# Layer 0 of a two-layer decoder trunk: plain block products on unnormalised inputs in its first two column groups, squares taken by rows, and four operand pairs of the output projection taken ahead

## The chip, the core and the metric

The kernel runs on one core of a Trainium2 chip. A core has five engines with a queue each: TensorE (PE in the profile, its weight loads PEld), VectorE (DVE), ScalarE (ACT), GpSimd (POOL) and SyncE (SP, which here only issues DMAs). Each works through its queue in order and waits on semaphores. The metric is the device time of one execution, in microseconds (us).

## The reference, cut to what matters

The input x has 1024 tokens of 1024 channels, in float32. Layer 0 normalises every token, projects to 4096 columns (2048 for pooling, 2048 for a gate), pools and mixes in four groups, gates, and projects back. Layer 1 is an attention layer that the change doesn't touch.

```python
def rms_norm(x, g):
    inv = lax.rsqrt(jnp.mean(x * x, axis=-1, keepdims=True) + RMS_EPS)
    return x * inv * g

def pooling_mixer(u, w_in, w_group, scale, w_out):
    xb, z = jnp.split(u @ w_in, 2, axis=-1)
    ...                                   # trailing means of 2, 4, 8, 16 tokens, minus self
    mixed = jnp.einsum('bsgi,gio->bsgo', pooled, w_group).reshape(B, S, D_INNER)
    return (mixed * scale * jax.nn.silu(z)) @ w_out
...
u = rms_norm(h, norm_g[0]); h = h + pooling_mixer(u, ...)
```

## The kernel before

Every float32 operand is split into a high and a low part of a faster matmul type (`split`, `u_split`): ACT copies the high part, DVE subtracts to get the low one. A 128x512 product is then three matmuls (`mm3`, lines 89 to 91): high by high, low by high, high by low.

Layer 0's input projection works on channels by tokens. The transposed x (`xt`) is cut into four blocks `B[j, l, kb]`: channel half j, token half l, and four tiles of 128 channels by 512 tokens in each. Two times 128 output columns make a `Group`; there are 16, eight for the pooled part and eight for the gate. A group is a 2 by 2 block product, done with seven block products of twelve matmuls each instead of eight, by the Strassen-Winograd scheme: the operands on the token side are `G[1]` and `G[2]` (two plain blocks of u), `G[3]` (a third) and `G[4]` to `G[7]` (sums and differences of blocks), those on the weight side are sums that POOL makes (lines 268 to 270 and 296). A sum of blocks that lie in different token halves needs u itself, with the norm factors in it.

The order at the start is therefore: `load_x(0)` loads the first token half, ACT squares each tile, TensorE adds up the squares over the channels by matmuls with a matrix of ones (line 155), POOL takes the power -1/2 (line 175), four transposes (line 178) spread the factors over the partitions, and `to_u` (line 186) multiplies. `first()` and `ahead()` then do products 1 and 2 of the four groups of the first gate and pool quarter (96 matmuls). `load_x(1)` does the second half; `u_sums` (lines 204, 205, 214, 220) makes the sums, half of them on POOL, and splits them. After that each `rest()` runs its five other products, evacuating product 1 on ACT (lines 246 and 276). Pooling (lines 314 to 323), the mixing products (`mixed`) and the stores to the DRAM tiles `yd` follow, row block by row block; the last stores go through one buffer, `old`, and POOL (lines 353 to 357).

The output projection is a 2 by 2 block product again, in a pool of tiles (`ob`) that opens when layer 0's pool closes. Its first product, `ops1`, needs `yd[1]`, complete since half of layer 0, but its loads stand behind the last stores on SP. `ops6`, the next product, needs three weight tiles per step and two sums of them on POOL (lines 452 and 453).

The Tile framework orders the instructions of each engine by a simulated timeline; the order of the code sets the priorities. PSUM has eight banks of 128x512 (`bank`).

Of the kernel before, what the change touches and what calls it, by code (L numbers as in the profile page):

```python
# [15 lines left out]
P = 128  # L16
S = 1024
# [28 lines left out]
def trunk(ctx, tc, x, xt, g, pw, pg, psc, pwo, sqk, sv, sz, swo, nf, out):  # L46
# [19 lines left out]
    ones = const.tile([P, 2], F32, name="ones")  # L66
    nc.gpsimd.memset(ones, 1.0)
# [56 lines left out]


# [6 lines left out]
    with tc.tile_pool(name="l0", bufs=2) as l0:  # L132
# [14 lines left out]
        def load_x(l, then={}):  # L147


            half = HALVES[l]  # L150
            ps = bank()

            def ssq(sq, first, last):
                for j in range(4):
                    nc.tensor.matmul(  # L155
                        ps[:, 2 * j:2 * j + 2], lhsT=sq[:, j * P:(j + 1) * P], rhs=ones,
                        start=first and j == 0, stop=last, skip_group_check=True)

            for k in range(NK):
                t = B[k // 4, l, k % 4] = pl_tile()  # L160
                nc.sync.dma_start(t, xt[k * P:(k + 1) * P, half * 512:half * 512 + 512])
                if k in then:
                    then[k]()
                sq = wide(k)[:, :512]
                act(sq, t, AF.Square)
                if l == 0:
                    ssq(sq, k == 0, k == NK - 1)
                elif k % 2:
                    nc.gpsimd.tensor_tensor(sq, sq, before, ALU.add)
                    ssq(sq, k == 1, k == NK - 1)  # L170
                before = sq
            ms = small.tile([P, 4], F32, name="ms4")
            nc.vector.tensor_scalar(ms, ps[:, 0:8:2], 1.0 / D, EPS, ALU.mult, ALU.add)
# [5 lines left out]
            rsb = l0.tile([P, 512], F32, name="w_raw", bufs=3)  # L179
            act(rsb, pt, AF.Copy)  # L180
            return rsb

        def to_u(k, l, rsb, n=None):
            j, kb = divmod(k, 4)
            t = B[j, l, kb]
            nc.vector.scalar_tensor_tensor(  # L186
                t, in0=t, scalar=g_sb[:, k:k + 1], in1=rsb, op0=ALU.mult, op1=ALU.mult)
            if n:
                u_split(n, kb, t)

        def u_split(n, kb, raw):
            hi, lo = u_tile(n, kb)
            act(hi, raw, AF.Copy)
            nc.vector.tensor_tensor(lo, raw, hi, ALU.subtract)

        def u_sums(rsb):

            t3 = []
            for kb in range(4):
                b11, b12, b22 = B[0, 0, kb], B[0, 1, kb], B[1, 1, kb]  # L200
                to_u(kb, 1, rsb)
                to_u(4 + kb, 1, rsb)
                t3.append(wide(kb)[:, :512])
                nc.vector.tensor_tensor(t3[kb], b22, b12, ALU.subtract)
                nc.gpsimd.tensor_tensor(b12, b11, b12, ALU.subtract)
                if kb:
                    t2(kb - 1, t3)
            t2(3, t3)
            for kb in range(4):
                u_split(7, kb, t3[kb])  # L210
            for kb in range(4):
                u_split(5, kb, B[0, 1, kb])
            for kb in range(4):
                nc.gpsimd.tensor_tensor(B[0, 0, kb], B[0, 0, kb], B[1, 0, kb], ALU.subtract)
                u_split(4, kb, B[0, 0, kb])
            for kb in range(4):
                u_split(3, kb, B[1, 1, kb])

        def t2(kb, t3):
            nc.vector.tensor_tensor(B[0, 0, kb], t3[kb], B[0, 0, kb], ALU.add)  # L220
            u_split(6, kb, B[0, 0, kb])
# [6 lines left out]
        def tmp():  # L228
            return l0.tile([P, 512], F32, name="avx", bufs=5)

        class Group:


            def __init__(self, c):
                self.c, self.a, self.early = c, {}, False
# [4 lines left out]
            def first(self):  # L240
                if (0, 0) not in self.a:
                    self.load(0, 0)
                self.p1 = bank()
                product(self.p1, split(self.a[0, 0]), 1)
                self.a1 = tmp()
                act(self.a1, self.p1, AF.Copy)

            def second(self):
                self.load(0, 1)
                product(self.p1, split(self.a[0, 1]), 2, True)  # L250

            def ahead(self):

                self.second()
                self.a, self.early = {}, True

            def rest(self, dst, fn):

                if self.early:
                    self.load(0, 0)  # L260
                else:
                    self.first()
# [9 lines left out]
                def out(i, l, in0, in1):  # L272
                    half = HALVES[l]
                    d = dst[i][:, half * 512:half * 512 + 512]
                    if in1 is None:
                        return act(d, in0, fn)
# [6 lines left out]
                v = self.a1  # L283
# [6 lines left out]
                if self.early:  # L290
# [607 lines left out]
```

## Time and profile before

| | us |
|---|---|
| median of 3 runs | 1623.95 (1623.34 to 1623.99) |
| the profiled execution | 1624.09 |
| its span in the trace | 1622.4 |
| PE busy | 1552.7 (96%) |
| DVE / ACT / POOL busy | 1120.4 / 674.0 / 399.6 |
| layer 0's input stage, to its last product with a token-side sum | 0 to 452 |
| output projection of layer 0 | 472 to about 640 |

PE is the busiest engine, so the time goes where PE stands idle or runs at half its clock. Views read: the share of busy time by slices, the list of what PE waited for, the timeline by engine, and tables of windows with the granted clock. A matmul's duration in the timeline overlaps its neighbours; its cost is the distance between two starts.

### The profile page before, as it was taken

To read this page: it belongs to the slowest core of one execution; us is meant where nothing else is said; L and a number is where in the kernel's file an instruction comes from. 1 tells how busy PE (TensorE), PEld (TensorE's weight loads), DVE (VectorE), ACT (ScalarE), POOL (GpSimd) and SP (SyncE) were. 2 spreads that over 40 slices of the span, in tenths; PEclk is the share of its full clock that TensorE was granted. 3 is DMA by queue.
4 is the path that set the end of the run, shared out by engine and by line. 5 is a ranking of instruction groups with operands and counts; after the bars stand their busy time and mean duration, and the time that the engine had idled before them with its cause. 6 is when DMAs were issued, how large, how long until landed. Compare 5 with 4: busy or idle time off the path is not lost.

```text
span 1622.4 us, 23428 instructions
## 1 busy us (share of the span) xinstructions
PE 1552.7 (96%) x8328; PEld 1336.8 (82%) x8328; DVE 1120.4 (69%) x1647; ACT 674.0 (42%) x1332; POOL 399.6 (25%) x826
## 2 busy tenths in 40 slices
PE   7399999999969998999999999999999999999997
PEld 7278888888857887888988988988988989989986
DVE  3597774958837687477667667657757757758678
ACT  6243332322324455355435435435335435435344
POOL 2562233254235252011102101101101102101113
PEclk9799999999979999999999999999999999999999
DMA  5113222143279742211021021021021021021012
GB/s 182 39 59 117 92 98 84 59 162 117 77 276 325 263 143 70 88 61 51 27 59 46 27 64 41 27 65 40 27 66 40 27 66 40 27 66 40 27 45 105
DMA packets 74358, 135.25 MB, mean 83 GB/s; under 512 B 8960, under 2 KB 8960, under 8 KB 74240
## 3 DMA queue, kind: packets, MB, share of 16 engines
q1 hardware_dynamic: 74096, 133.74, 25.4%
q8 instruction: 66, 1.08, 0.3%
q14 instruction: 52, 0.43, 0.1%
q10 hardware_dynamic: 144, 0.01, 0.0%
HBM read 104.35 MB, written 20.97 MB: 77 GB/s over the span
## 4 chain that ended last, share of the span: by engine, by line
PE 88%; DVE 5%; issue 2%; POOL 2%; ACT 1%; DMA 1%; SPq 0%; POOLq 0%; DVEq 0%; ACTq 0%
PE pd L89 15%; PE pd L91 14%; PE pd L90 14%; PE bk L89 10%; PE bk L90 10%; PE bk L91 10%; PE pt L727 4%; PE po L89 2%; PE po L90 2%; PE po L91 2%; PE pq L683 2%; PE pq L684 2%; PE bk L155 1%; DVE pl L186 1%; DVE w_lo L99 1%
## 5 line engine op out<-in xcount | busy, mean ns | idle before, releaser
L695 DVE TENSOR_TENSOR_SCAN om<-om 128x257 f32<-128x257 f32 (+1 forms) x192 | 187.0, 978 | 80.5 <-POOL om L692 34.6
L89 PE MATMUL pd<-slot,w_hi 128*128 128x512 f32 x512 | 202.4, 395 | 4.1 <-DVE slot L506 4.0
L90 PE MATMUL pd<-slot,w_hi 128*128 128x512 f32 x512 | 202.0, 394 | 0.0
L91 PE MATMUL pd<-slot,w_lo 128*128 128x512 f32 x512 | 200.3, 392 | 0.0
L99 DVE TENSOR_TENSOR w_lo<-w_raw,w_hi 128x512 fp32r<-128x512 f32 x196 | 141.3, 728 | 82.1 <-ACT w_hi L98 77.9
L98 ACT ACTIVATE w_hi<-w_raw 128x512 fp32r<-128x512 f32 x196 | 122.4, 629 | 135.4 <-PE pd L90 77.6
L688 ACT ACTIVATE om<-pq 128x256 f32<-128x256 f32 (+1 forms) x192 | 94.3, 491 | 169.0 <-PE pq L684 162.1
L89 PE MATMUL pd<-w_hi,slot 128*128 128x256 f32 x512 | 146.3, 286 | 0.0
L91 PE MATMUL pd<-w_hi,slot 128*128 128x256 f32 x512 | 144.6, 283 | 0.0
L90 PE MATMUL pd<-w_lo,slot 128*128 128x256 f32 x512 | 144.3, 282 | 0.0
L692 POOL TENSOR_SCALAR_AFFINE_SELECT om<-om 128x128 f32<-128x128 f32 x128 | 48.8, 384 | 374.5 <-ACT om L688 371.8
L98 ACT ACTIVATE w_hi<-a_raw 128x512 fp32r<-128x512 f32 x96 | 59.8, 629 | 150.1 <-PE bk L90 88.0
L89 PEld LDWEIGHTS pd<-slot,w_hi 128*128 128x128 f32 x512 | 96.6, 189 | 22.7 <-DVE slot L506 4.3
L731 DVE TENSOR_TENSOR at_l<-pt,at_h 128x512 fp32r<-128x512 f32 (+1 forms) x160 | 99.4, 625 | 21.1 <-ACT at_h L730 20.9
L730 ACT ACTIVATE at_h<-pt 128x512 fp32r<-128x512 f32 (+1 forms) x160 | 86.6, 552 | 63.8 <-PE pt L727 63.1
L91 PEld LDWEIGHTS pd<-slot,w_lo 128*128 128x128 f32 x512 | 96.6, 189 | 19.9 <-DVE w_lo L99 0.4
L90 PEld LDWEIGHTS pd<-slot,w_hi 128*128 128x128 f32 x512 | 96.6, 189 | 18.4
L699 DVE TENSOR_TENSOR om<-pq,om 128x256 f32<-128x256 f32 (+1 forms) x192 | 104.7, 551 | 9.0 <-DVE t L753 0.2
L89 PE MATMUL pd<-w_hi,y_h 128*128 128x512 f32 x256 | 107.0, 418 | 0.4 <-ACT y_h L756 0.4
L99 DVE TENSOR_TENSOR w_lo<-a_raw,w_hi 128x512 fp32r<-128x512 f32 x96 | 75.4, 788 | 39.1 <-ACT w_hi L98 39.1
L90 PE MATMUL pd<-w_lo,y_h 128*128 128x512 f32 x256 | 102.1, 399 | 0.0
L91 PE MATMUL pd<-w_hi,y_l 128*128 128x512 f32 x256 | 100.3, 395 | 0.0
(185 smaller groups left out, 4043.3 us busy)
## 6 DMA issues: line engine op xcount, KB each, us to landing
a_raw<-in_pw SPq DMA_DIRECT2D x72, 256.0 KB, 3.0
w_raw<-in_pwo SPq DMA_DIRECT2D x72, 256.0 KB, 4.6
y_raw<-y_dram SPq DMA_DIRECT2D x56, 256.0 KB, 4.0
y_dram<-t SPq DMA_DIRECT2D x48, 256.0 KB, 2.1
w_raw<-in_sqk SPq DMA_DIRECT2D x34, 256.0 KB, 2.8
w_raw<-in_sz SPq DMA_DIRECT2D x34, 256.0 KB, 3.2
w_raw<-in_sv SPq DMA_DIRECT2D x32, 256.0 KB, 2.7
w_raw<-in_swo SPq DMA_DIRECT2D x32, 256.0 KB, 2.6
```

The costliest lines, as they stand in the source:

```text
L89: nc.tensor.matmul(ps, lhsT=lh, rhs=rh, start=start, stop=False, skip_group_check=more)
L90: nc.tensor.matmul(ps, lhsT=lh, rhs=rl, start=False, stop=False, skip_group_check=more)
L91: nc.tensor.matmul(ps, lhsT=ll, rhs=rh, start=False, stop=stop, skip_group_check=more)
L98: act(hi, raw, AF.Copy)
L99: nc.vector.tensor_tensor(lo, raw, hi, ALU.subtract)
L688: act(om[:, 1:1 + n], pz, AF.Sigmoid, scale=-ZSCALE)
L692: nc.gpsimd.affine_select(out=om[:, 1:1 + P], in_=om[:, 1:1 + P], pattern=[[1, P]], base=0, channel_multiplier=-1, compare_op=ALU.is_gt, f ...
L695: nc.vector.tensor_tensor_scan(out=om[:, :1 + n], data0=om[:, :1 + n], data1=om[:, :1 + n], initial=1.0 if s.first else carry[r], op0=ALU. ...
L699: nc.vector.tensor_tensor(om[:, :n], pz, om[:, :n], ALU.mult)
L727: nc.tensor.transpose(tp[:, c * P:(c + 1) * P], om[:, (j - b0) * P:(j - b0 + 1) * P], ident)
L730: act(ah[:, :n], tp[:, :n], AF.Copy)
L731: nc.vector.tensor_tensor(al[:, :n], tp[:, :n], ah[:, :n], ALU.subtract)
```

## The change

- The first two groups, `Group(0)` (pool) and `Group(16)` (gate), are done as eight plain block products, four column tiles `c1` on the first token half and four (`c2`) on the second. They take `xt` times the weight `g` of each channel, without the norm factors; the factors are put on when the result leaves PSUM (`scaled`, on DVE). The weights of these groups stay split in tiles that `G[5]` and `G[7]` take over later; the second half's operands stand in `G[4]` and `G[3]` until the true ones come.
- `G[1]` and `G[2]` stay without norm factors for all groups. Product 1 is evacuated by DVE with a multiplication by the factors `rsb[0]` instead of by ACT as a copy, and so is the result of products 1 and 2.
- The sums of squares are taken from x by rows, with ACT's accumulator (`factors`), in place of 96 small matmuls with ones; the four x tiles of each half are loaded a second time for that, 512 KB each.
- The sums of `u_sums` are all made on DVE, none on POOL.
- Half of the first product of the output projection (row blocks 0 to 3, 48 matmuls) is done inside layer 0's last quarter.

```diff
+        def factors(l):
+            ssq = small.tile([P, 4], F32, name="ssq4")
+            for j in range(4):
+                t = wide(j)[:, :D]
+                nc.sync.dma_start(t, xv[4 * HALVES[l] + j])
+                act(t, t, AF.Square, accum_out=ssq[:, j:j + 1])
             rs = small.tile([P, 4], F32, name="rs4")
-            nc.gpsimd.tensor_tensor(rs, ms, mhalf.broadcast_to([P, 4]), ALU.pow)
+            nc.gpsimd.tensor_scalar(rs, ssq, 1.0 / D, EPS, ALU.mult, ALU.add)
+            nc.gpsimd.tensor_tensor(rs, rs, mhalf.broadcast_to([P, 4]), ALU.pow)
             pt = bank()
             for j in range(4):
                 nc.tensor.transpose(pt[:, j * P:(j + 1) * P], rs[:, j:j + 1].broadcast_to([P, P]), ident)
...
+        def scaled(d, ps, l, fn):
+            d = d[:, HALVES[l] * 512:HALVES[l] * 512 + 512]
+            nc.vector.tensor_tensor(d, ps, rsb[l], ALU.mult)
+            if fn != AF.Copy:
+                act(d, d, fn)
...
-                    self.first()
+                self.load(0, 0)
+                p1 = bank()
+                product(p1, split(self.a[0, 0]), 1)
+                v = tmp()
+                nc.vector.tensor_tensor(v, p1, rsb[0], ALU.mult)
...
+        c1 = {(a, i): bank() for a in range(2) for i in range(2)}
+        for j in range(2):
+            first_w(j)
+            for k in range(4 * j, 4 * j + 4):
+                for a, i in c1:
+                    first_mm(c1[a, i], a, i, k, (1, 2))
+        factors(0)
+        for k in range(NK):
+            load_xt(k, 1, (4, 3)[k // 4])
+        factors(1)
+        c2 = {}
+        for a in range(2):
+            for i in range(2):
+                ps = c2[a, i] = bank()
+                for k in range(NK):
+                    first_mm(ps, a, i, k, (4, 3))
...
+                if gi == 3 and op == 1:
+                    y1 = []
+                    for kb in range(4):
+                        t = wide(kb)
+                        raw, hi = t[:, :512], t[:, 512:S].bitcast(F32R)
+                        nc.sync.dma_start(raw, yd[1][kb])
+                        split_to((hi, raw.bitcast(F32R)), raw)
+                        y1.append((hi, raw.bitcast(F32R)))
...
+                    if gi == 3 and op + i == 2:
+                        pa = [bank() for _ in range(4)]
+                        out_product(pa, lambda kb: (
+                            split(raw_of(pwo[kb][:, :512], l0, "a_raw", bufs=6)), y1[kb]), kbs=range(4))
                     mixed(gi, 2 * op + i, pooled, dst[i])
...
-        out_product(pa, ops1)
+        out_product(pa, ops1, kbs=range(4, 8))
```

In numbers of large matmuls (128x512), layer 0's input and mixing stages had 16 x 84 + 768 = 2112 and now have 14 x 84 + 2 x 96 + 768 = 2136; the 96 with ones are gone.

**PE's queue where the factors of the second token half come in.** Before, the transposes of the second half's factors (`rs_455`) follow the 96 products of `first` and `ahead` and some of the matmuls with ones, and the next product takes the sums of u (`g_0h` is here a part of `G[6]` or `G[7]`):

```order
L90 MATMUL bk<-g_3l,w_hi 128x512
L91 MATMUL bk<-g_3h,w_lo 128x512
L155 MATMUL bk<-ones,xb 128x2 x5
L178 MATMUL bk<-ident,rs_455 128x128 x4
L89 MATMUL bk<-g_0h,w_hi 128x512 x2
L90 MATMUL bk<-g_0l,w_hi 128x512
```

Now the factors of both halves are transposed behind the 96 products of `c1`, and the next product is the first of the 96 of `c2`, on `xt` alone:

```order
L88 MATMUL bk<-g_3l,g_3h 128x512
L89 MATMUL bk<-g_3h,g_3l 128x512
L184 MATMUL bk<-ident,rs_335 128x128 x4
L184 MATMUL bk<-ident,rs_406 128x128 x4
L87 MATMUL bk<-g_0h 128x512
L88 MATMUL bk<-g_0l,g_0h 128x512
```

So 192 large matmuls stand ahead of the first one that needs u, where 96 stood; `c2` itself needs no factor but stands behind the transposes of `rs_406`.

**DVE's queue up to the first weight split of the next group.** `w_lo<-a_raw` is the low part of a weight sum that product 6 waits for; before, the sums of u alternate with their splits (L194), and half of them come from POOL:

```order
L220 TENSOR_TENSOR pl<-xb,pl 128x512
L194 TENSOR_TENSOR g_3l<-pl,g_3h 128x512
L194 TENSOR_TENSOR g_0l<-pl,g_0h 128x512
L194 TENSOR_TENSOR g_1l<-pl,g_1h 128x512
L194 TENSOR_TENSOR g_2l<-pl,g_2h 128x512
L194 TENSOR_TENSOR g_3l<-pl,g_3h 128x512
L99 TENSOR_TENSOR w_lo<-a_raw,w_hi 128x512 x2
```

Now the same queue holds the evacuations of `c1` and `c2` (L207), pooling of the first two tiles (L273 to L276) and the sums on u (L369 to L371, L387) as well:

```order
L276 SCALAR_TENSOR_TENSOR wsum<-wsum,xb 128x1024
L157 TENSOR_TENSOR g_3l<-pl,g_3h 128x512
L157 TENSOR_TENSOR g_2l<-pl,g_2h 128x512
L387 TENSOR_TENSOR pl<-pl 128x512
L157 TENSOR_TENSOR g_0l<-pl,g_0h 128x512
L157 TENSOR_TENSOR g_1l<-pl,g_1h 128x512
L275 TENSOR_TENSOR wsum<-wsum,ratio_82 128x1
L207 TENSOR_TENSOR t_570<-bk,w_raw 128x512
L157 TENSOR_TENSOR g_2l<-pl,g_2h 128x512
L387 TENSOR_TENSOR pl<-pl 128x512
L97 TENSOR_TENSOR w_lo<-a_raw,w_hi 128x512
```

That `w_lo`, the last row, now stands 58 instructions behind the first multiplication of x by the factors.

**PE's queue at the end of layer 0.** Before, the rest of the mixing products (`pl`) stands behind the last product with `G[3]`, 23 matmuls to the first one of the output projection:

```order
L90 MATMUL bk<-g_3l,w_hi 128x512
L91 MATMUL bk<-g_3h,w_lo 128x512
L91 MATMUL bk<-pl,w_lo 128x512 x2
L89 MATMUL bk<-pl,w_hi 128x512
L90 MATMUL bk<-pl,w_hi 128x512
L91 MATMUL bk<-pl,w_lo 128x512
```

Now the products taken ahead (`wsum` and `xb` hold their row blocks) follow it, 27 of the 48, and then 24 mixing products; the other 21 stand in front of it:

```order
L87 MATMUL bk<-g_3h,w_hi 128x512
L88 MATMUL bk<-g_3l,w_hi 128x512
L89 MATMUL bk<-g_3h,w_lo 128x512
L87 MATMUL bk<-w_hi,wsum 128x512
L88 MATMUL bk<-w_lo,wsum 128x512
L89 MATMUL bk<-w_hi,wsum 128x512
L87 MATMUL bk<-w_hi,xb 128x512
```

51 products in place of 23 stand between the last product with `G[3]` and the first one on loads of the output projection.

## Rows read from the trace of the kernel before

**Rows 1.** The page's busy times; what PE waited for, 0 to 560 us.
```profile
PE 1552.7 (96%) x8328; PEld 1336.8 (82%) x8328; DVE 1120.4 (69%) x1647; ACT 674.0 (42%) x1332; POOL 399.6 (25%) x826
...
PE bk L89 <- ACT g_0h L193: 27.6, 2, 25.5
```

**Rows 2.** Timeline of PE: start, duration, instruction, count, idle before.
```profile
4.89 1.84 PE L155 MATMUL bk<-ones,wsum 128*128 128x2 f32 x8 [4.89 <-ACT wsum L165]
...
33.28 0.63 PE L89 MATMUL bk<-g_1h,w_hi 128*128 128x512 f32 x1
33.70 0.63 PE L90 MATMUL bk<-g_1l,w_hi 128*128 128x512 f32 x1
...
55.44 0.65 PE L178 MATMUL bk<-ident,rs 128*128 128x128 f32 x4 [1.36 <-POOL rs L175]
81.57 1.22 PE L89 MATMUL bk<-g_0h,w_hi 128*128 128x512 f32 x2 [25.48 <-ACT g_0h L193]
...
85.58 0.40 PE L90 MATMUL bk<-g_0l,w_hi 128*128 128x512 f32 x1
```

**Rows 3.** Windows: length, busy by engine, granted clock, DMA share, GB/s.
```profile
10.00:15.00 5.00, 5.00 (x25) 5.00 (x25) 2.06 (x3) 3.48 (x6) 0.00 (x0) 1.00 1.05 395
...
55.00:60.00 5.00, 0.65 (x4) 0.41 (x4) 3.25 (x2) 0.60 (x1) 4.76 (x5) 0.83 0.00 0
60.00:65.00 5.00, 0.00 (x0) 0.00 (x0) 5.00 (x7) 3.10 (x6) 1.29 (x1) 0.50 0.01 2
```

**Rows 4.** Timeline of ACT at the start.
```profile
4.14 0.61 ACT L165 ACTIVATE wsum<-pl 128x512 f32<-128x512 f32 x1
...
15.94 0.63 ACT L165 ACTIVATE wsum<-pl 128x512 f32<-128x512 f32 x1 [2.17 <-DMA pl<-in_xt]
```

**Rows 5.** Timeline of POOL, 18 to 106 us.
```profile
18.96 1.03 POOL L175 TENSOR_TENSOR rs<-ms,mhalf 128x4 f32<-128x4 f32 x1 [0.35 <-DVE ms L173]
...
65.83 11.16 POOL L205 TENSOR_TENSOR pl<-pl 128x512 f32<-128x512 f32 x3 [4.54 <-DVE wsum L204]
```

**Rows 6.** Timeline of DVE, 18 to 125 us.
```profile
21.83 5.39 DVE L186 SCALAR_TENSOR_TENSOR pl<-pl,g_sb,w_raw 128x512 f32<-128x512 f32 x8 [2.95 <-ACT w_raw L180]
...
65.67 0.68 DVE L194 TENSOR_TENSOR g_0l<-pl,g_0h 128x512 fp32r<-128x512 f32 x1
66.28 0.68 DVE L204 TENSOR_TENSOR xb<-pl 128x512 f32<-128x512 f32 x1
...
75.80 1.75 DVE L194 TENSOR_TENSOR g_0l<-wsum,g_0h 128x512 fp32r<-128x512 f32 x1
77.47 1.75 DVE L194 TENSOR_TENSOR g_1l<-xb,g_1h 128x512 fp32r<-128x512 f32 x1
...
108.12 2.34 DVE L314 TENSOR_TENSOR wsum<-xb 128x1024 f32<-128x1024 f32 x2
...
111.17 4.59 DVE L317 SCALAR_TENSOR_TENSOR wsum<-wsum,xb 128x1024 f32<-128x1024 f32 x2
```

**Rows 7.** PE's first and last large matmul of the stretch without a wait.
```profile
122.92 0.50 PE L89 MATMUL bk<-g_0h,w_hi 128*128 128x512 f32 x1 [0.28 <-DVE avx L287]
...
452.05 0.39 PE L91 MATMUL bk<-g_3h,w_lo 128*128 128x512 f32 x1
```

**Rows 8.** Window of 40 us with the busiest DVE, columns as in rows 3.
```profile
280.00:320.00 40.00, 40.00 (x178) 33.14 (x177) 38.50 (x45) 14.53 (x26) 14.07 (x11) 1.00 0.21 66
```

**Rows 9.** Timeline, all engines, from the last product to the output projection.
```profile
466.73 0.42 SPq L104 DMA_DIRECT2D w_raw<-in_pwo  x1
...
471.96 2.07 PE L89 MATMUL bk<-w_hi,y_hi 128*128 128x512 f32 x4 [14.31 <-ACT y_hi L98]
```

**Rows 10.** The output projection's first product and `ops6`: window, POOL's sums, PE's wait.
```profile
500.00:505.00 5.00, 5.00 (x23) 3.83 (x21) 2.78 (x4) 2.05 (x4) 1.73 (x3) 1.00 1.05 388
...
518.26 1.62 POOL L453 TENSOR_TENSOR s<-s,w_raw 128x512 f32<-128x512 f32 x1
...
506.71 1.21 PE L89 MATMUL bk<-w_hi,y_hi 128*128 128x512 f32 x4 [1.67 <-ACT w_hi L98]
```

More of the change, by code (lines that the diff above doesn't have):

```diff
@@ L123, in trunk, with out_product @@
     HALVES = (1, 0)
+    def out_product(ps, operands, more=False, kbs=range(8)):
+        for kb in kbs:
+            (wh, wl), (yh, yl) = operands(kb)
+            for t in range(4):
+                ts_ = slice(t * P, (t + 1) * P)
+                mm3(ps[t], yh[:, ts_], yl[:, ts_], wh, wl, kb == 0 and not more, kb == 7, more)
     ps_ctx = ExitStack()
@@ L145, in wide, with split_to @@
             return l0.tile([P, S + 16], F32, name="xb" if i % 2 else "wsum")
[L147 to L173, printed above, removed]
+        def split_to(t, raw, scale=None):
+            hi, lo = t
+            if scale is None:
+                act(hi, raw, AF.Copy)
+                nc.vector.tensor_tensor(lo, raw, hi, ALU.subtract)
+            else:
+                act(hi, raw, AF.Copy, scale=scale)
+                nc.vector.scalar_tensor_tensor(lo, in0=raw, scalar=scale, in1=hi, op0=ALU.mult, op1=ALU.subtract)
@@ L186, in to_u @@
             nc.vector.scalar_tensor_tensor(
-                t, in0=t, scalar=g_sb[:, k:k + 1], in1=rsb, op0=ALU.mult, op1=ALU.mult)
-            if n:
-                u_split(n, kb, t)
+                t, in0=t, scalar=g_sb[:, k:k + 1], in1=rsb[l], op0=ALU.mult, op1=ALU.mult)
         def u_split(n, kb, raw):
[L192 to L221, printed above, removed]
+            split_to(u_tile(n, kb), raw)
         def product(ps, w, n, more=False):
@@ L289, in rest @@
                 out(1, 1, x_, p5)
-                if self.early:
-                    self.load(0, 1)
-                else:
-                    self.second()
-                out(0, 0, self.p1, None)
+                self.load(0, 1)
+                product(p1, split(self.a[0, 1]), 2, True)
+                scaled(dst[0], p1, 0, fn)
                 a12 = self.a[0, 1]
@@ new lines, in trunk, with first_w @@
+        fw = {}
+        def first_w(j):
+            for a, c in enumerate(first):
+                for i in range(2):
+                    raw = raw_of(pw[c + i][:, j * 512:j * 512 + 512], l0, "a_raw", bufs=6)
+                    n = (7, 5)[a]
+                    t = fw[a, i, j] = tuple(
+                        l0.tile([P, 512], F32R, name=f"g{n}_{2 * i + j}{x_}", bufs=1) for x_ in "hl")
+                    split_to(t, raw)
+                    if j == 0:
+                        load_xt(2 * a + i, 0, 1)
+                    else:
+                        load_xt(4 + 2 * a + i, 0, 2)
@@ L375, in trunk @@
+        for kb in range(4):
+            dve(B[0, 0, kb], B[0, 0, kb], B[1, 0, kb], ALU.subtract)
+            u_split(4, kb, B[0, 0, kb])
+        for kb in range(4):
+            u_split(3, kb, B[1, 1, kb])
         for gi in range(len(WINDOWS)):
             pooled = {}
-            if gi:
-                xs = [Group(gi * 4), Group(gi * 4 + 2)]
-                zs = [Group(16 + gi * 4), Group(16 + gi * 4 + 2)]
             for cp in range(2):
-                dst = [xb_tile() for _ in range(2)]
-                xs[cp].rest(dst, AF.Copy)
+                if gi + cp:
+                    dst = [xb_tile("old" if gi == 0 and i else "xb", 2 - (gi == 0 and i)) for i in range(2)]
+                    Group(gi * 4 + 2 * cp).rest(dst, AF.Copy)
+                else:
+                    dst = firsts[0]
@@ L411, in ysplit @@
             return split(raw_of(yd[n][kb], ob, "y_raw"), ob, "y")
-        def out_product(ps, operands, more=False):
-            for kb in range(8):
-                (wh, wl), (yh, yl) = operands(kb)
-                for t in range(4):
-                    ts_ = slice(t * P, (t + 1) * P)
-                    mm3(ps[t], yh[:, ts_], yl[:, ts_], wh, wl, kb == 0 and not more, kb == 7, more)
         def tmp2(name):
@@ L438, in ops1 @@
             return split(wload(0, 0, kb)), ysplit(1, kb)
-        pa = [bank() for _ in range(4)]
-        out_product(pa, ops1)
+        out_product(pa, ops1, kbs=range(4, 8))
         a1 = []
```

97 lines of the change are left out of this document (51 added, 46 removed).

## The prediction, made before the changed kernel ran

> **What bounds the kernel now.** I read the busy times first: PE is busy 96% of the span [rows 1], so the change can only win where PE stands idle, runs at half clock, or does matmuls that go away. The list of waits shows where that is: PE loses 27.6 us to the first split of u, 25.5 of it in one wait [rows 1], and 14.3 us to the first operand of the output projection [rows 9]; between 122.92 and 452.05 it has no wait worth a term. PE's timeline tells the start: sums of squares from 4.89 on, 96 large products up to about 54 (55.44 less the 1.36 of its wait), and then nothing until 81.57, while DVE and POOL make the sums of u [rows 2]. The reader should see three paces there: a large matmul every 0.43 us at the half clock (from 33.28 to 33.70) [rows 2], every 0.227 us at the full one (1450 matmuls by the order between 122.92 and 452.05, 329.13 / 1450) [rows 7], and a granted clock that falls to 0.50 soon after PE stops (0.83 in the 5 us in which it stops) and comes back about 4 us after it resumes [rows 2, 3]. DVE has two paces as well: 0.61 us from start to start alone, 1.67 us while POOL adds tiles (the three of 11.16 us and the ones behind them) [rows 5, 6].
>
> **The first products (gain).** They need a weight tile, an x tile and their splits, no factor. ACT can start at 4.14 [rows 4]; two copies of 0.63 give PE a start near 5.5. The 16 tiles have 256 KB each; before, the 17th tile of that size is there at 15.94 [rows 4], so the last lands near 15, and ACT (0.63 a copy) and DVE (0.61) keep up. PE is the slower: about 12 products at half clock (5 us), then 84 x 0.227 = 19.1. I put the end of `c1` at 30.
>
> **The wait for the factors (loss).** `c2` stands behind the transposes of both factors. The x tiles by rows are the last of 40 times 256 KB: 17 by 15.9, the other 23 at 395 GB/s [rows 3], 0.66 each, so about 31. ACT, in order, waits with three of the four squares behind the copy of the first factors, which waits for transposes behind `c1`. So from 30: transposes 0.65 [rows 2], copy 0.6, three squares, POOL's power 1.03 [rows 5] and a small multiplication, transposes 0.65. A 128x1024 square with the accumulator isn't shown; between the 0.63 of a 128x512 one [rows 4] and twice that plus a read of the accumulator lies 0.6 to 1.45; I take 1.3, since the time of such copies goes with their columns, so 3.9 (1.9 to 4.4). With handoffs 7.3: `c2` starts at 37.3, at half clock, as after the stop at 54. 96 x 0.227 = 21.8 and about 2.2 for ten products at half clock: its end is 61.5. The ones-matmuls that go, from 4.89 on [rows 2], lay where PE had nothing else; that gain is in the start at 5.5 and isn't counted again.
>
> **DVE's queue (where the stall goes).** PE could go on at 61.5, but the weight split `w_lo` of product 6 is late. From the first multiplication by factors, at 31.3, to the weight split that the mixing of the first group needs stand 80 DVE instructions: 16 with a scalar at 0.67 (5.39 for 8), four of 1024 columns at 1.17 to 2.3 (I take 1.2, since the larger one ran beside POOL), two tiny of 0.2, and 58 at 0.60 [rows 6]: 10.7 + 4.8 + 0.4 + 34.8 = 50.7. Seven weight sums on POOL lie in that stretch; at 1.67 for the instructions that they slow, against 0.61, I add half of seven times 1.06, 3.6 (0 to 7.4). DVE is there at 85.6. PE waits for it about 5 us at product 6, runs some products at half clock again, waits 1 to 2 us more before the mixing, and has done its 282nd large product by 91. The first rival says what it is without DVE.
>
> [...]
>
> **The rest of layer 0.** By the order of before, the 255th large product starts at 122.92 and the 1705th, the last with `G[3]`, at 452.05. Now the 283rd starts at 91 and the 1749th is 1466 x 0.227 = 332.8 later: 423.8, a gain of 28.3, with the 24 added products and the 21 taken ahead paid in it. 14 groups put two evacuations each on DVE that ACT did: 28 x 0.6 = 17 us of DVE's time, hidden where DVE is idle. It is 38.5 of 40 us busy at worst [rows 8]; two groups a stretch of that length put in 2.4, so there they overflow by about 1. I take 1.5 lost (0 to 8).
>
> **The output projection.** The chain behind the last `G[3]` product doesn't change: silu, scale, POOL, store, reload through `old`, POOL, and only then SP's loads, 14.7 us after it (466.73), and PE's first product, 19.9 after it (471.96) [rows 7, 9]. 51 products, 11.6 us, fill that time in place of 23; the last mixing products are done before POOL wants them, so the chain isn't longer. After it 48 products fewer are left, 10.9 us. But that stage is fed by DMA: 388 GB/s in `ops6`, with PE waiting for its weight sums (1.67 us) [rows 10], and POOL's last sum ends at 519.9, 53.2 us after the first load. With four steps less, 8 loads of 256 KB go, 2.1 MB, 5.4 us at 388 GB/s; POOL's and PE's work comes earlier by no more than this. So 5.4 is the ceiling, not 10.9; with PE waiting more, and cooler, I take 4.5 (0 to 6).
>
> **The sum.** 28.3 - 1.5 + 4.5 = 31.3 off the profiled execution's 1624.09 gives 1592.8; the median of the runs lies 0.14 lower: **1592.6**.
>
> **Rivals.** *DVE doesn't hold PE:* the multiplications and splits keep ahead, and the 90 products behind `c2` run from 61.5 at 0.227, to 82 in place of 91: 1583.6. For it: PE's own order has 18 products between `c2` and the first need; against: 58 instructions in front of it. *DVE holds it longer:* 1.67 us for more than seven instructions and 2.3 for the wide ones, or the weight loads late behind `a_raw` tiles that hold sums of u until DVE has read them (SP waits there in order): 12 us more, 1604.6. *The output projection gains nothing*, since what it waits for is DMA and POOL: 1597.1, inside the main range. *Slower:* product 1 is evacuated by DVE in order, and PE, which adds product 2 onto the same bank, waits for it; with a wide operation in front (2.3 us) [rows 6] at each of 28 evacuations, 64 us are lost, 1656. It decides from 1.2 us per evacuation on (32.8 / 28). Against it: PE does 36 products, 8 us, between the two, and it waited for DVE nowhere in this stretch with DVE at 38.5 of 40 [rows 8]. *The change doesn't do what it says:* PE's work can't start before the factors anyway. The order speaks against it, since `c1` stands first on PE.
>
> **How the numbers follow.** Forecast, with the output projection's rival inside it: 0.66. DVE not holding: 0.12. DVE holding longer: 0.15. Slower: 0.03. No start ahead of the factors, near 1620: 0.04, half within 0.2%. The range is the forecast with the bounds of its terms: low 1592.6 - 9 (no hold by DVE) - 1.5 - 0.9 = 1581; high 1592.6 + 4 + 6.5 + 1.4 = 1604.5 with half of the longer hold inside. About 0.2% (3.2 us) is what a measurement of this kernel can tell from no change. Faster 0.95, same 0.02, slower 0.03.
>
> **What would show it right or wrong.** In the profile after: PE's first large matmul near 5.5, `c1` ended near 30, a gap of 6 to 7 us with eight transposes, `c2` from 37 to 61, a wait of some 5 us on `w_lo` near 66 to 71, no PE wait of length from 95 to 424, a gap of 8 us before the output projection, and PE waits in `ops6`. It is wrong if PE is idle beyond 95, if waits on lines 226 or 207 show up between 100 and 420, or if `ops6` ends more than 6 us earlier or later against the last `G[3]` product than I put it.

## The result, and the profile of the changed kernel

The changed kernel takes 1601.74 us (median of 4 runs, 1599.34 to 1602.63) against 1623.64 in the same rounds: a ratio of 0.9866, with an interval of 0.9848 to 0.9883. That is 21.9 us less, where 31.3 was forecast; the time lies in the upper part of the range. The profiled execution took 1599.34 us (span 1597.3), 24.75 less than the profiled execution before, and the steps are judged on that pair. It is the changed kernel's fastest execution, 2.4 us below its median, so the pair shows 2.9 us more than the medians do.

What PE waited for up to 700 us (in total, times, longest), as in [rows 1]:

```profile
PE bk L87 <- ACT y_hi L96: 14.1, 1, 14.1
PE bk L87 <- ACT w_hi L96: 10.3, 4, 4.2
PE bk L184 <- POOL rs L181: 6.3, 1, 6.3
PE bk L87 <- ACT g_0h L159: 5.4, 1, 5.4
PE bk L89 <- DVE w_lo L97: 5.4, 1, 5.4
PE pd L87 <- ACT w_hi L96: 2.3, 1, 2.3
```

The 25.5 us behind the sums of u have become three shorter waits (6.3, 5.4 and 4.2, the last one inside the second line). The first line is the gap ahead of the output projection, as long as before [rows 9]. The other three waits of the second line lie in the output projection, where one of 1.7 stood before [rows 10].

PE's timeline in the same form as [rows 2] and [rows 7]: its first large product, the last one of `c2`, the waits, the last product with `G[3]`, the output projection, the last transposes, layer 1:

```profile
5.44 0.80 PE L87 MATMUL bk<-g_0h 128*128 128x512 f32 x1 [5.44 <-ACT g_0h L159]
...
36.44 1.12 PE L184 MATMUL bk<-ident,rs 128*128 128x128 f32 x4 [6.33 <-POOL rs L181]
...
60.33 0.39 PE L89 MATMUL bk<-g_3h,g_3l 128*128 128x512 f32 x1
...
70.62 0.80 PE L89 MATMUL bk<-g_0h,w_lo 128*128 128x512 f32 x1 [5.41 <-DVE w_lo L97]
...
86.46 0.80 PE L87 MATMUL bk<-pl,w_hi 128*128 128x512 f32 x1 [4.24 <-ACT w_hi L96]
...
95.75 0.39 PE L89 MATMUL bk<-pl,w_lo 128*128 128x512 f32 x1
...
429.14 0.39 PE L89 MATMUL bk<-g_3h,w_lo 128*128 128x512 f32 x1
...
455.33 2.07 PE L87 MATMUL bk<-w_hi,y_hi 128*128 128x512 f32 x4 [14.12 <-ACT y_hi L96]
...
616.72 5.80 PE L525 MATMUL bk<-ident,s 128*128 128x128 f32 x32 [2.12 <-DVE s L521]
...
624.78 0.50 PE L87 MATMUL pd<-slot,w_hi 128*128 128x512 f32 x1 [2.26 <-ACT w_hi L96]
```

Up to 82 us this is the forecast. The wait at 86.46 is not in it. In the windows of the waits at 70.62 and 86.46 the granted clock was 0.55 and 0.50 (columns as in [rows 3]):

```profile
70.00:75.00 5.00, 4.38 (x11) 3.53 (x12) 5.00 (x9) 1.89 (x3) 0.00 (x0) 0.55 0.29 89
...
85.00:90.00 5.00, 3.54 (x8) 2.81 (x9) 4.08 (x7) 2.19 (x4) 0.23 (x1) 0.50 0.49 168
```

The last transposes and the first product of layer 1 in the kernel before:

```profile
638.10 5.80 PE L501 MATMUL bk<-ident,s 128*128 128x128 f32 x32 [2.12 <-DVE s L497]
...
647.93 0.50 PE L89 MATMUL pd<-slot,w_hi 128*128 128x512 f32 x1 [4.03 <-DVE slot L506]
```

So the gain at the last product with `G[3]` is 452.05 - 429.14 = 22.9, at the last 32 transposes 638.10 - 616.72 = 21.4, and at the first product of layer 1 647.93 - 624.78 = 23.2. From the `G[3]` product to the transposes the change *lost* 1.5 us; behind them it won 3.4, which no step spoke of.

### The profile page after: what moved, and what is told of

Same layout as the page of the kernel before. It is cut to its first block, busy times and chain, and to the rows that moved or that the text cites. A ratio compares the mean times of both kernels' runs of the same rounds, so it can differ in the third digit from the quotient of the medians.

```text
span 1597.3 us, 23281 instructions
## 1 busy us (share of the span) xinstructions
PE 1539.7 (96%) x8256; PEld 1322.8 (83%) x8256; DVE 1131.8 (71%) x1681; ACT 663.1 (42%) x1310; POOL 362.6 (23%) x807
## 3 DMA queue, kind: packets, MB, share of 16 engines
q8 instruction: 65, 1.06, 0.3%
## 4 chain that ended last, share of the span: by engine, by line
PE 67%; DMA 4%; DVE 3%; POOL 1%; ACT 1%; issue 1%; SPq 0%; POOLq 0%; DVEq 0%; ACTq 0%
PE pd L89 15%; PE pd L87 15%; PE pd L88 15%; PE pt L751 4%; PE bk L88 3%; PE bk L89 2%; PE bk L87 2%; PE po L87 2%; PE po L88 2%; PE po L89 2%; PE pq L707 2%; PE pq L708 2%; DMA w_raw<-in_pwo 1%; DVE wsum L273 1%; DMA y_raw<-y_dram 1%
## 5 line engine op out<-in xcount | busy, mean ns | idle before, releaser
L97 DVE TENSOR_TENSOR w_lo<-w_raw,w_hi 128x512 fp32r<-128x512 f32 x190 | 135.7, 722 | 77.4 <-ACT w_hi L96 72.8
L96 ACT ACTIVATE w_hi<-w_raw 128x512 fp32r<-128x512 f32 x190 | 118.6, 628 | 141.1 <-PE pd L88 74.1
L96 ACT ACTIVATE w_hi<-a_raw 128x512 fp32r<-128x512 f32 x88 | 54.6, 628 | 151.8 <-PE bk L88 90.2
L88 PEld LDWEIGHTS pd<-w_lo,slot 128*128 128x128 f32 x512 | 97.5, 190 | 0.8
```

The lines of the kernel that those rows point to most:

```text
L88: nc.tensor.matmul(ps, lhsT=lh, rhs=rl, start=False, stop=False, skip_group_check=more)
```

## The experiments

The table has the medians of the timed runs, the ratio to the kernel before, and four landmarks of the profiled execution: the 283rd large product, the last product with `G[3]`, the last block of transposes, and the first product of layer 1. Between executions of equal code the landmarks move by one to three us (the last product with `G[3]` stands at 429.14 in the changed kernel and at 427.58 in e9, which differs from it behind that place only; at 423.62 in e8 and 426.79 in e10), so late landmarks are compared by their distances. The last product with `G[3]` is not the same place everywhere: it is the 1705th large product before and in e5, with 23 more up to the output projection, the 1744th in e1, e6 and e11, with 8 more, and the 1749th in the others, with 51 more. A distance from it holds different work in each of the three.

| kernel | median us | ratio (interval) | 283rd | last `G[3]` | transposes | layer 1 |
|---|---|---|---|---|---|---|
| before | 1623.6 | | | 452.05 | 638.10 | 647.93 |
| changed | 1601.74 | 0.9866 (0.9848 to 0.9883) | 95.75 | 429.14 | 616.72 | 624.78 |
| e1 | 1605.67 | 0.9888 (0.9872 to 0.9905) | 96.85 | 429.33 | 617.67 | 631.91 |
| e2 | 1603.30 | 0.9877 (0.9863 to 0.9892) | 95.41 | 428.21 | 612.68 | 626.89 |
| e3 | 1593.93 | 0.9816 (0.9801 to 0.9830) | 91.03 | 424.33 | 609.86 | 617.92 |
| e4 | 1598.63 | 0.9847 (0.9833 to 0.9862) | 92.71 | 425.97 | 616.13 | 624.19 |
| e5 | 1621.23 | 0.9990 (0.9981 to 0.9998) | | 450.36 | 636.07 | 644.13 |
| e6 | 1600.68 | 0.9862 (0.9848 to 0.9875) | 95.51 | 427.18 | 616.12 | 624.19 |
| e7 | 1592.57 | 0.9811 (0.9798 to 0.9824) | 90.11 | 424.56 | 608.94 | 617.01 |
| e8 | 1585.84 | 0.9771 (0.9758 to 0.9784) | 89.19 | 423.62 | 602.03 | 610.11 |
| e9 | 1601.45 | 0.9866 (0.9853 to 0.9880) | 94.84 | 427.58 | 617.67 | 626.00 |
| e10 | 1587.52 | 0.9782 (0.9769 to 0.9796) | 91.59 | 426.79 | 606.55 | 614.61 |
| e11 | 1589.02 | 0.9789 (0.9776 to 0.9802) | 89.99 | 423.27 | 603.93 | 612.01 |
| e12 | 1597.99 | 0.9848 (0.9835 to 0.9862) | 94.52 | 428.28 | 613.30 | 623.14 |

### The start: what made the wait at 86.46 (e3, e4, e7, e12)

What SP's queue waited for in the changed kernel between 20 and 100 us, longest first:

```profile
SPq L102 <- DVE pl L371: 28.6, 4, 27.2
SPq L102 <- DVE t L207: 11.9, 1, 11.9
SPq L102 <- DVE w_lo L97: 11.3, 5, 5.5
```

SP stood 27.2 us before one weight load, until DVE had read the first tile of `t3` for the last time (line 371): `t3` lies in tiles of `a_raw`. Behind it SP stood another 11.9 us, before a load into the tile `w_raw` that holds the second half's factors until line 207 has read them. The loads for the next weight sums went out from 73.04 on, and POOL and ACT show what came of it:

```profile
76.21 5.68 POOL L232 TENSOR_TENSOR w_raw<-a_raw 128x512 f32<-128x512 f32 x1 [10.95 <-DMA a_raw<-in_pw]
81.97 1.59 POOL L233 TENSOR_TENSOR a_raw<-a_raw 128x512 f32<-128x512 f32 x1
...
83.57 1.66 POOL L255 TENSOR_TENSOR a_raw<-a_raw 128x512 f32<-128x512 f32 x1
```

```profile
85.26 0.63 ACT L96 ACTIVATE w_hi<-a_raw 128x512 fp32r<-128x512 f32 x1 [6.29 <-POOL a_raw L255]
85.79 1.13 ACT L96 ACTIVATE w_hi<-w_raw 128x512 fp32r<-128x512 f32 x2
```

PE wanted the second row's split, of a weight tile with no sum in it, but ACT works in order and waited 6.29 us for the sum of the first row. DVE itself was through its list at 84.1.

**e3: `t3` in other tiles.**

```diff
-            t3.append(l0.tile([P, 512], F32, name="a_raw", bufs=6))
+            t3.append(tmp())
```

> The changed kernel, with the four sums t3 in the tiles avx, so that SP can load the next groups' weights into a_raw while DVE still reads t3. If the wait of 4.2 us before the first mixing product (86.46) comes from weight loads that stand behind t3's tiles: that wait goes, with the half clock behind it, the next group's 283rd large product starts near 91 in place of 95.5, and the time is 4 to 5 us shorter. If DVE's queue alone holds PE there, PE's wait is as long as before, the 283rd large product within 1 us of 95.5, and the time the same.

The 283rd large product starts at 91.03, the forecast's 91 (94.84 to 96.85 in the changed kernel and the four with its start: e1, e2, e6, e9), and the median falls by 7.8 us, where 4 to 5 had been expected. What PE still waited for from 60 to 100 us:

```profile
PE bk L89 <- DVE w_lo L97: 1.2, 1, 1.2
PE bk L88 <- DVE g_3l L157: 0.9, 1, 0.9
PE bk L87 <- ACT w_hi L96: 0.4, 1, 0.4
```

The first theory holds. It cost something too: SP puts weight loads in front of the last x tiles, so the second transposes come at 40.42 in place of 36.44. The profiled executions differ by 7.2 us. 4.8 of them are there at the last `G[3]` product and 2.1 come between it and the transposes, where PE's waits in the output projection are 5.6 us in place of 7.2; whether the edit or the spread between executions makes these 2.1, no run shows.

**e4: the transposes of the second half's factors inside `c2`.**

```diff
...
                 ps = c2[a, i] = bank()
                 for k in range(NK):
                     first_mm(ps, a, i, k, (4, 3))
+                if a + i == 0:
+                    spread(1, rs1)
```

> The changed kernel, with the transposes of the second half's factors behind the first 24 matmuls of c2 instead of in front of all of them, so that PE has work while ACT squares and POOL takes the power. If DVE's queue sets when layer 0 gets going (the prediction's step): c2 ends 6 us earlier, near 54, PE then waits as much longer for the weight split of product 6, and the 283rd large product starts within 1 us of 95.5. If PE is what binds, it starts 6 us earlier and the time is 6 us shorter.

Neither held. `c2` ends at 52, 8.4 us earlier, and PE then waits 9.1 us in one piece in place of 5.4, for ACT's copy of a weight tile; the 283rd product comes 3.0 us earlier. ACT's queue has that copy behind one of a sum of u, which DVE had ready at 64.0, and POOL's weight sum, whose load had waited 30.4 us for the tiles of `t3`, was done at 63.4. This run can't tell DVE and the loads apart; e7 can.

**e7: e2, e3 and e4 together.** (e2 stands below.)

> The changed kernel with the edits of e2, e3 and e4 together: products taken ahead behind the last mixing, t3 in other tiles, transposes of the second half's factors inside c2. Layer 1's first product takes bank 0, freed by the third of the eight transposed tiles, as in the changed kernel. If the three gains lie in different places: e3's 7.8 us, 3 us of e4, and e2's 4 us at the transposes add up to 13 to 15 us, near 1587. If DVE's queue is what holds layer 0's start once the loads are early, e4's part goes under: PE waits again for a split behind c2, and the time is near 1590.

The second theory held, and e2's part went under too: from the 283rd product to the transposes e7 and e3 both need 518.8 us. The last matmul of `c2` starts at 59.87 where it starts at 63.98 in e3, but PE then waits 3.2 us for the split of `g_0h`, and the last `G[3]` product is at 424.56 against 424.33. ACT's copy in that split had waited for a sum on DVE (line 376). DVE is the reason, in a window of e7 (columns as in [rows 3]):

```profile
50.00:90.00 40.00, 34.92 (x136) 26.75 (x135) 40.00 (x62) 17.89 (x31) 10.74 (x6) 0.91 0.15 46
```

DVE is busy 40.00 of 40 us with 62 instructions. With the loads early, DVE's list is the bound of this stretch, as the prediction said.

**e12: as e7, with four of the sums of u on POOL, as before the change.**

```diff
-        dve(B[0, 0, kb], B[0, 0, kb], B[1, 0, kb], ALU.subtract)
+        nc.gpsimd.tensor_tensor(B[0, 0, kb], B[0, 0, kb], B[1, 0, kb], ALU.subtract)
```

> As e7, with the last four sums of u (those for G[4]) on POOL, as before the change, instead of on DVE. DVE is busy without a break from 50 to 90 us in e3 and e7. If DVE's count of instructions sets the pace: four less are 2.4 us, so the last product with G[3] comes up to 2.4 us earlier. If POOL's sums slow DVE by 1.06 us each (1.67 for 0.61, as in the kernel before): 4.2 us more than gained 2.4, so about 2 us later, and POOL's weight sums come later as well.

The last `G[3]` product comes 3.7 us later than in e7, the 283rd product at 94.52, where it starts at 89.19 to 91.59 in the four kernels with the sums on DVE (e7, e8, e10, e11). That is the second theory, with more lost than its 2 us. The same window, and DVE and POOL beside each other, in e12:

```profile
50.00:90.00 40.00, 31.76 (x122) 24.41 (x121) 40.00 (x55) 17.95 (x31) 16.10 (x9) 0.88 0.12 40
```

```profile
41.40 1.27 POOL L235 TENSOR_TENSOR w_raw<-a_raw 128x512 f32<-128x512 f32 x1
...
69.68 5.20 POOL L235 TENSOR_TENSOR w_raw<-a_raw 128x512 f32<-128x512 f32 x1 [12.60 <-DVE t L210]
74.95 2.29 POOL L236 TENSOR_TENSOR a_raw<-a_raw 128x512 f32<-128x512 f32 x1
...
77.25 5.07 POOL L392 TENSOR_TENSOR pl<-pl 128x512 f32<-128x512 f32 x3
```

```profile
76.02 0.68 DVE L229 TENSOR_TENSOR avx<-bk,rsb 128x512 f32<-128x512 f32 x1
...
77.72 1.77 DVE L157 TENSOR_TENSOR g_2l<-pl,g_2h 128x512 fp32r<-128x512 f32 x1
79.42 1.78 DVE L97 TENSOR_TENSOR w_lo<-a_raw,w_hi 128x512 fp32r<-128x512 f32 x1
```

DVE is as busy as in e7, but gets through 55 instructions in place of 62: four of them, beside POOL's sums of u, took 1.75 to 1.78 us in place of 0.68. The other way round, POOL's sum at 69.68 took 5.20 us while DVE kept its pace, 0.68 to 0.69 an instruction. The number of inputs in SBUF doesn't tell here which instruction is slowed: beside POOL's sum at 74.95 the evacuation at 76.02, which reads PSUM and one tile in SBUF, took 0.68, and a DVE instruction with two inputs in SBUF at 75.42 took 0.68 as well. What decides whether DVE or POOL is slowed was not shown. The median is 5.4 us above e7; about 2 of them are a wait at layer 1 (4.0 in place of 2.3, below).

### The end of layer 0 and the output projection (e1, e2, e6, e8 to e11)

**e1: nothing taken ahead.**

```diff
-                        pa = [bank() for _ in range(4)]
-                        out_product(pa, lambda kb: (
-                            split(raw_of(pwo[kb][:, :512], l0, "a_raw", bufs=6)), y1[kb]), kbs=range(4))
...
-        out_product(pa, ops1, kbs=range(4, 8))
+        pa = [bank() for _ in range(4)]
+        out_product(pa, ops1)
```

> The changed kernel, but all eight steps of the output projection's first product stand behind layer 0, as before; nothing is taken ahead. The prediction's step (taking ahead gains 4.5 us): the transposes behind the output projection start 4 to 5 us later than the 616.7 us of the changed kernel, and the time is about 1606. The theory from the changed kernel's trace: taking ahead lost there, since its 48 matmuls stand in front of the last mixing products and lengthen the chain from the last product with G[3] to SP's loads (21.1 us against 14.7 before). Then without it the last product with G[3] comes 21 x 0.227 = 4.8 us earlier, at 424.4, the first product of the output projection 20 to 23 us behind it, near 446, and the transposes 166 us behind that, near 612: 3 to 6 us faster than the changed kernel.

Neither theory held. The last `G[3]` product stands at 429.33 and not at 424.4: only 5 large products fewer come in front of it, not 21, since the scheduler moved mixing products there. The time, 3.9 us up, looks like the prediction's 4.5. The landmarks say otherwise: the transposes are only 1 us later, and the rest is a longer wait in front of layer 1's first product, 8.42 us in place of 2.26:

```profile
631.91 0.80 PE L87 MATMUL pd<-slot,w_hi 128*128 128x512 f32 x1 [8.42 <-DVE slot L518]
```

This product doesn't need the tile that it waits for here. By the program's allocation it takes PSUM bank 0 over from the pool that closes, and the eight last transposed tiles rotate through the banks: in e1 bank 0 is read last by the eighth of them, in the kernel before by the fifth, in the changed kernel by the third. Which one it is depends on the order in which banks were taken all through layer 0. The traces agree: the product starts at 631.91 in e1, where the eighth evacuation ends at 631.86, and at 647.93 in the kernel before, where the fifth ends at 647.87.

**e5: the kernel before, and e6: e1, each with layer 1's pools opened in another order,** so that the first product takes bank 1, which the first of the eight tiles frees.

```diff
+    ps_o = ctx.enter_context(tc.tile_pool(name="ps_o", bufs=1, space=PSUM, reuse_waits="tile"))
     ps_d = ctx.enter_context(tc.tile_pool(name="ps_d", bufs=3, space=PSUM, reuse_waits="tile"))
...
-    ps_o = ctx.enter_context(tc.tile_pool(name="ps_o", bufs=1, space=PSUM, reuse_waits="tile"))
```

> The kernel before, with one line moved: the pool of one bank (ps_o) is opened ahead of ps_d, so that layer 1's first product pd lies in bank 1 instead of bank 0. Bank 0 is read last by the fifth of the eight last transposed tiles, bank 1 by the first of them. If layer 1's first product waits for the evacuation of the bank that it takes over: its wait of 4.0 us falls to the 2.3 us that its weight split needs, as in the changed kernel, PE doesn't fall to the half clock behind it, and the time is 2 to 4 us shorter than before. If the wait is for its operands, nothing changes.

> As e1 (nothing of the output projection taken ahead), with ps_o opened ahead of ps_d: layer 1's first product then takes bank 1, which the first of the eight last transposed tiles frees, in place of bank 0, which the last of them frees. If e1's wait of 8.4 us there comes from the bank: it falls to 2.3, and the time is 6 to 7 us shorter than e1. What is left against the changed kernel is then what taking ahead is worth by itself: the transposes stood 1 us later in e1, so within 1 to 2 us of the changed kernel; by the prediction's step 4.5 us slower than it.

Layer 1's first product in e5 and in e6:

```profile
644.13 0.50 PE L89 MATMUL pd<-slot,w_hi 128*128 128x512 f32 x1 [2.26 <-ACT w_hi L98]
```

```profile
624.19 0.80 PE L87 MATMUL pd<-slot,w_hi 128*128 128x512 f32 x1 [2.27 <-ACT w_hi L96]
```

Both fall to 2.3 us. The kernel before gains 2.1 us by the median (its interval ends at 0.9998), e1 gains 5.0 (6 to 7 had been expected). So the bank theory holds, and e6, with nothing taken ahead, stands at 1600.68 against 1601.74: taking ahead is worth nothing that can be measured in this kernel. From the 283rd large product to the transposes, the same work in both, e6 needs 520.6 us and the changed kernel 521.0. The 48 products taken ahead bring the output projection's first product 6.4 us later (359.6 us behind the 283rd in place of 353.2) and shorten the way from it to the transposes by 6.1 us (161.4 in place of 167.5), not by the 10.9 us of their work.

**e2: the products taken ahead behind the last mixing products.**

```diff
                 for i in range(2):
-                    if gi == 3 and op + i == 2:
-                        pa = [bank() for _ in range(4)]
...
                     mixed(gi, 2 * op + i, pooled, dst[i])
+                if gi == 3 and op == 1:
+                    pa = [bank() for _ in range(4)]
+                    out_product(pa, lambda kb: (
```

> The changed kernel, with the 48 matmuls taken ahead placed behind the last mixing products instead of in front of them. If the order of PE's queue alone lengthened the chain: the last product with G[3] at 424.4, SP's loads 14.7 us behind it (439) in place of 450.2, the gap of PE before the output projection about 9 us in place of 14.1, and the time 8 to 11 us shorter. If the chain of stores through the one old buffer and the two t buffers sets the pace whatever PE does (four row blocks at 8 to 9 us each): loads 5 to 6 us earlier and the time about as much shorter. If the output projection is fed by DMA alone, as the prediction said, the waits in ops6 stay (7 us in the changed kernel).

The first product of the output projection comes 25.1 us behind the last `G[3]` product, where the changed kernel has 26.2 and the kernel before 19.9. So the place in PE's queue accounts for 1.1 of the 6.3 us by which the chain grew, and none of the times expected came. PE's waits in `ops6` stay, at 6.0 us, as the third theory said. The transposes are 4.0 us earlier than in the changed kernel; the wait of 8.4 us at layer 1 (bank 0 is freed by the eighth tile here as well) takes that back.

Part of the rest shows on DVE at the end of layer 0. The changed kernel first, then the kernel before:

```profile
432.82 0.69 DVE L207 TENSOR_TENSOR t<-bk,rsb 128x512 f32<-128x512 f32 x1 [6.06 <-DMA y_dram<-t]
```

```profile
452.54 0.69 DVE L277 TENSOR_TENSOR t<-bk,avx 128x512 f32<-128x512 f32 x1 [6.14 <-PE bk L91]
```

Before, the last group's evacuation waits for PE; now it waits 6.06 us for a store, since its tile `t` is one of two and the row block two places earlier isn't out. The chain through `old` (POOL, store, reload, POOL) sets the end; moving PE's last products changes it by 1.0 us (e2). From POOL's first step of the last four row blocks to the output projection it takes 34.3 us before (437.67 to 471.96), 34.9 in e1 (415.40 to 450.33), 37.4 in e2 and 38.4 in the changed kernel (416.94 to 455.33). The 2.5 to 3.5 us that taking ahead adds to e1's time lie in several small waits; a single cause wasn't found.

**e8: as e7, with the loads of x for the residual held back.**

```diff
+        if after is not None:
+            nc.vector.tensor_copy(h[t, n][:, :1], after[:, :1])
         nc.sync.dma_start(h[t, n], xv[t][:, n * 512:n * 512 + 512])
...
-            load_h(t, 0)
+            load_h(t, 0, v[0])
...
```

> As e7, with twelve loads of x for the residual (256 KB each) held back by a one-column DVE write until ops6 has ended; in the changed kernel they lie between 459 and 477 us, between the weights of ops6. If DMA feeds ops6, as the prediction said: 12 x 256 KB are 3.1 MB, 8 us at 388 GB/s; the waits in ops6 (7 us and a half clock behind them in the changed kernel) fall to under 2 us, and the time is 5 to 8 us shorter than e7. If POOL's sums or the store of the last rows bind there, it is the same within 2 us.

6.7 us faster than e7, as the first theory said. PE's waits from 440 to 560 us, in e7 and in e8:

```profile
PE bk L87 <- ACT w_hi L96: 5.0, 2, 3.3
PE bk L88 <- DVE w_lo L97: 1.3, 2, 0.6
```

```profile
PE bk L88 <- DVE w_lo L97: 1.1, 3, 0.4
PE bk L87 <- ACT w_hi L96: 1.0, 1, 1.0
```

The same window of both, e7 first (columns as in [rows 3]; the last one is what DMA moved, in GB/s):

```profile
460.00:465.00 5.00, 5.00 (x24) 4.14 (x23) 3.26 (x4) 3.84 (x7) 2.95 (x2) 1.00 1.06 388
```

```profile
460.00:465.00 5.00, 5.00 (x24) 4.14 (x23) 4.39 (x5) 3.92 (x9) 3.47 (x3) 1.00 0.76 210
```

From 460 to 480 us DMA moved 386 GB/s in e7, about as much as the 388 in [rows 10], and 295 in e8. So DMA feeds `ops6`, and 12 loads that nobody needs yet took 3.1 MB of it. Whether their bytes cost the time or their places between the weight loads in SP's queue, the run doesn't separate. At 1585.84 us e8 is the fastest kernel of the study, 15.9 us below the changed one.

**e9: ops1's loads on ACT's queue; e10: the same on e8; e11: e10 with nothing taken ahead.** (e11 has the first four steps' loads on ACT's queue.)

```diff
...
-            return split(wload(0, 0, kb)), ysplit(1, kb)
+            return split(wload(0, 0, kb, nc.scalar)), ysplit(1, kb, nc.scalar)
```

> The changed kernel with one thing moved: the eight loads of ops1 (weights and yd[1]) are issued from ACT's queue instead of SP's, where they stand behind the last stores of layer 0. yd[1] is complete since half of layer 0. If the gap of 14.1 us before the output projection comes from the order of SP's queue: ACT is free of the last evacuations at 434.8, the loads go out there instead of at 450.2, ops1 follows the last mixing product (440.8) with a gap under 3 us, and the time is 5 to 10 us shorter, the rest going into ops6, whose operands still come behind the stores. If the tiles of ob can't be had before layer 0's last tiles are free, the gap stays.

> As e8 (products behind the last mixing, t3 apart, transposes inside c2, x loads late), with ops1's eight loads on ACT's queue as in e9. If both hold: the gap of 12.9 us before the output projection shrinks below 4, ops6 starts as early as its own operands allow, near 449, and the time is 5 to 9 us shorter than e8's 1585.8, near 1579.

> As e10, but with nothing of the output projection taken ahead: all eight steps of ops1 stand behind layer 0, the first four steps' loads on ACT's queue. If taking ahead only fills a gap that the order of SP's queue makes, 96 products (21.8 us) fill the same time, and the time is within 2 us of e10. If it is worth the 4.5 us of the prediction by itself, because 16 loads less stand in the DMA-fed stage, it is 4 us or more slower than e10.

e9 keeps the gap (15.1 us) and the time, but it is no clean test of SP's order: SP now issues seven loads of x from 448.46 on, while `ops1`'s last operands are still to come. In e10 the loads of x are held back; the gap is 11.3 us where e8 has 12.9, and PE's waits in `ops6` grow from 2.1 to 5.1 us. So the order of SP's queue accounts for at most 1.6 us of the gap, which had been expected to fall below 4. The gap in e10:

```profile
450.35 2.07 PE L87 MATMUL bk<-w_hi,y_hi 128*128 128x512 f32 x4 [11.32 <-ACT y_hi L96]
```

In e9 ACT's last evacuation starts at 432.66, but its loads go out late and one by one:

```profile
440.77 0.33 ACTq L102 DMA_DIRECT2D w_raw<-in_pwo  x1
444.57 0.34 ACTq L102 DMA_DIRECT2D y_raw<-y_dram  x1
446.29 0.33 ACTq L102 DMA_DIRECT2D w_raw<-in_pwo  x1
```

The tiles of the output projection lie on tiles of layer 0 (by the allocation, `y_raw` on the `wsum` and `xb` that hold the row blocks taken ahead), which fits the second theory; which tile each load waited for wasn't settled. e10 and e11 stand 1.5 us apart, within e10's "within 2 us": a second time taking ahead is worth at most that. e10 is no faster than e8, where 5 to 9 us had been expected.

## Why the prediction was right in its sign and 9 us too low

- **First products.** Right: PE starts at 5.44 (5.5), and the 96th product ends at 29.7 (30).
- **Wait for the factors.** Right: the wide square took 1.06 us and its read 0.19, together 1.25 (1.3); `c2` starts at 37.21 (37.3) and ends at 60.7 (61.5).
- **DVE's queue.** The count was right: DVE had done its list at 84.1 (85.6), and PE waited 5.41 us for product 6's split (5). The step that failed is the next clause, "waits 1 to 2 us more before the mixing": it was 4.24 us with eleven products 0.43 us apart behind it (granted clock 0.50 from 85 to 90 us), and the 283rd product came at 95.75 in place of 91. The mechanism is the one that the rival "DVE holds it longer" named and priced at 12 us, weight loads late behind `a_raw` tiles; it was worth 4.7 (e3). What the prediction priced only for DVE, the time that it loses beside POOL, hit POOL as well, as its own [rows 5] show (three sums in 11.16 us): one sum on the way to that wait took 5.68 us, where the one at 41.40 in e12, beside an idle DVE, takes 1.27.
- **The rest of layer 0.** Right: 1466 products in 333.4 us (332.8 + 1.5). The pace was read from a count two too high: in the trace the product at 122.92 is the 257th and not the 255th, which gives 329.13 / 1448 = 0.2273 each and 333.2 for the 1466. So the evacuations cost next to nothing. PE waits for none of lines 226 and 207 there; its one wait, 0.7 us, is for line 239, and the kernel before waits 0.5 us in that stretch for its line 277, which does the same. The rival "slower" had nothing to it. Gain at the last `G[3]` product: 22.9 where 26.8 was forecast.
- **The output projection.** Wrong: 4.5 us were forecast, 1.5 were lost, and the gap in front of it is 14.1 us where 8 were forecast. The rival "gains nothing" is what the runs bear out (e6). Two claims fell. "The chain isn't longer" rested on the last mixing products being early, but the chain waits for the stores through `old` and `t`, and grew from 19.9 to 26.2 us; what in taking ahead lengthens it stays open in part (e2). And the ceiling of 5.4 from 8 loads less took no account of 12 loads of x: before, they went out from 477 on, while `ops1` had 96 products to do; with 48 they fall into `ops6`, whose waits grew from 2.4 to 7.2 us. 10.9 us of work less, 6.3 of chain and 4.8 of waits more leave about nothing; the other 1.3 us fit the lower clock behind the waits (granted 0.63, 0.69, 0.99, 0.50 and 0.82 in the windows of 2.5 us from 480.0 to 492.5; before, 0.77 and 0.55 in those from 507.5 to 512.5). That DMA feeds this stage was right (e8).
- **Not in the sum.** 3.4 us won behind the transposes. 1.8 of them are the bank of layer 1's first product (9.83 us from transposes to product before, 8.06 now); the rest is the clock behind it (granted 0.79 in the 8 us from 647 before, 1.00 in those from 624 now) and the spread of layer 1 between executions, which these runs don't separate. No term of the prediction held this gain: that it brought the time nearer to the forecast is luck.

Together: 31.3 - 3.9 - 6.0 + 3.4 = 24.8, the 24.75 of the two profiled executions; the medians' 21.9 is 2.9 less, which is spread between executions that no step here explains.

## What to carry to other kernels

Before work is moved forward, follow the buffers that it borrows: here the tiles lent to `t3` held one weight load for 27.2 us, and everything behind it in SP's queue. Where a stage is fed by DMA, count all loads that fall into its time, and not its own alone (12 loads of x in `ops6`: 6.7 us, e8 against e7). When an edit changes how many tiles were taken or in which order, look at the first wait behind the next change of pools before its time is put down to the edit itself (8.42 us in e1 where the changed kernel has 2.26).

## What the runs showed that was not expected

- The wait at a change of PSUM pools follows the rotation of banks: 2.3, 4.0 and 8.4 us in front of the same product, by whether the third, fifth or eighth of eight evacuations frees its bank. In e1 and e2 it hid or mimicked the effect of the edit.
- POOL's sum of 128x512 took 1.27 us alone and 5.2, 5.7 and (in e4) 9.4 us beside a busy DVE; DVE's instruction took 0.68 alone and up to 1.78 beside POOL.
- The 48 products taken ahead, 10.9 us of work, brought nothing: what they saved behind the start of the output projection (6.1 us) they cost in front of it (6.4 us).
